# A transformer block in float32r pairs: the low parts of the feed-forward input weights come from an adding transfer instead of a subtraction

## The chip, the cores and the metric

The kernel runs on one core of a Trainium2 chip. A core has TensorE (PE, with its weight loads as PEld), VectorE (DVE), ScalarE (ACT), GpSimd (POOL) and SyncE (SP), which work from their own instruction queues, and 16 DMA engines. The metric is device time in microseconds: before the change the median of 3 runs is 1236.16 us (1234.19 to 1237.01).

## The reference

One block on 512 tokens with 1024 features in float32: a modulated norm, two kinds of attention (stick-breaking, retention), their gated mix, and a feed-forward part. The part that the change concerns:

```
hffn = modulate(rmsnorm(x, g_norm2[l]), shift2, scale2)
a, u = jnp.split(jnp.einsum('bsd,df->bsf', hffn, w_ffn_in[l]), 2, axis=-1)
x = x + gate2[:, None, :] * jnp.einsum('bsf,fd->bsd', jax.nn.silu(a) * u, w_ffn_out[l])
```

Each of a and u has 2816 columns, 22 tiles of 128.

## The kernel before, in words

Every large product is made of three matmuls for each tile. Weights and activations are split into a high part that fits the matmul's format (float32r) and a low part, the rest; `mm3` adds high x high, high x low and low x high. `gemm` does this for the 8 row tiles of a weight tile, which makes 24 matmuls in the order high, high, low for each row tile.

A weight tile is 128 x 1024 numbers (8 row tiles of 128 columns, 512 KB), packed on the host. `weight` (L204) fetches it: `load_raw` (L189) has SyncE's queue issue the load into one of three `raw` buffers; `split` (L194) has ACT copy raw to `whi` with rounding (L196), and DVE subtract, raw - whi, to `wlo` (L198). There are three buffers of `whi` and three of `wlo`, so a tile can be prepared only when PE has finished the third tile before it; the raw buffer comes free when both parts are made, and only then SyncE can issue the next load, in order.

The feed-forward part (the last loop of the kernel) runs in three chunks of 8, 8 and 6 tile pairs. For each pair i it fetches the tiles ("fa", i) and ("fu", i), here called fa and fu with the number, makes the products a and u in two of four PSUM banks, and `ff_act` makes Silu(a) x u: Silu on ACT (L764), the multiplication on DVE (L765), and the split into high and low activations, ACT then DVE (L196, L198). After each chunk come 8 products with w_ffn_out, whose tiles are fetched by `weight` too. Pair 0 runs by halves of 256 tokens, since the norm ahead of it (`norm2`, L753 to L757, and the reciprocal square root at L298 to L302) finishes the first half earlier than the second. Just before that, `add_residual` holds all three weight buffers until its last three tiles are done with both halves.

The order of instructions on each engine is made by the framework's scheduler, which moves what is ready sooner ahead; waits between engines are semaphores that it sets. GpSimd has work only in the earlier parts of the kernel.

Of the kernel before, what the change touches and what calls it, by code (L numbers as in the profile page):

```python
# [19 lines left out]
P = 128  # L20
# [17 lines left out]


def weight_plan():  # L40
    """(key, source, first row, row tiles, columns) of each packed weight tile, in order of use."""
    plan = []

    def add(key, src, r0, nk, cols):
        plan.append((key, src, r0, nk, cols))

    def rng(a, n):
        return [(a, n)]

    for kt in range(KT):  # L50
        add(("start", kt), "w_in", kt * P, 1, [(C_RQ, 256), (C_RK, 256), (C_RV, 256)])
    for g in range(4):
        for half in range(2):
            add(("sv", g, half), "w_in", half * 512, 4, rng(C_V + g * 256, 256))
        for p in (2 * g, 2 * g + 1):
            add(("sq", p), "w_in", 0, 8, rng(C_Q + p * P, P))
            add(("sk", p), "w_in", 0, 8, rng(C_K + p * P, P))
    for h in range(RH):
        for i in range(2):
            add(("rq", h, i), "w_in", 0, 8, rng(C_RQ + h * RK + i * P, P))  # L60
        for i in range(2):
            add(("rk", h, i), "w_in", 0, 8, rng(C_RK + h * RK + i * P, P))
        for i in range(2):
            for half in range(2):
                add(("rv", h, i, half), "w_in", half * 512, 4, rng(C_RV + h * RV + i * 256, 256))
        for i in range(4):
            add(("rg", h, i), "w_in", 0, 8, rng(C_RG + h * RV + i * P, P))
        for i in range(4):
            add(("pr", h, i), "w_proj_ret", h * RV, 4, rng(i * 256, 256))
    for i in range(8):  # L70
        add(("ps", i), "w_proj_sb", 0, 8, rng(i * P, P))
    for i in range(16):
        add(("br", i), "w_in", 0, 8, rng(C_BR + i * P, P))
    for i in range(8):
        add(("wo", i), "w_out", 0, 8, rng(i * P, P))
    for i in range(NF):
        add(("fa", i), "w_ffn_in", 0, 8, rng(i * P, P))
        add(("fu", i), "w_ffn_in", 0, 8, rng(DFF + i * P, P))
    for c, (k0, nk) in enumerate(FF_CHUNKS):
        for i in range(8):  # L80
            add(("fo", c, i), "w_ffn_out", k0 * P, nk, rng(i * P, P))
    return plan
# [4 lines left out]
PLAN = weight_plan()  # L87
WIDX = {e[0]: n for n, e in enumerate(PLAN)}

# column pairs of w_ada in order of use: (shift1, scale1) x 8, gate1 x 4, (shift2, scale2) x 8, gate2 x 4  # L90
ADA = (
    [(j, 8 + j) for j in range(8)]
    + [(16 + 2 * i, 17 + 2 * i) for i in range(4)]
# [1 line left out]
    + [(40 + 2 * i, 41 + 2 * i) for i in range(4)]  # L95
)

# smalls: columns of the packed small vectors
SM_BADA, SM_G1, SM_G2, SM_GF, SM_BB, SM_N = 0, 48, 56, 64, 72, 88

# (bank, column in the bank, first token, width) of the score block of 128 sources
GEO = ((0, 0, 0, 512), (1, 0, 128, 384), (2, 0, 256, 256), (2, 256, 256, 256))
BANKW = (512, 384, 512)

# [2 lines left out]
def kernel(  # L107
# [45 lines left out]
    def f(ap):  # L153
        return ap.bitcast(F32)

# [1 line left out]
    NCON = 2 * P + 48  # L157
    con = cpool.tile([P, NCON], F32, name="con")

# [25 lines left out]
    negones = cpool.tile([P, P], F32R, name="negones")  # L185
    nc.vector.tensor_scalar_mul(negones, ones, -1.0)

# [1 line left out]
    def load_raw(src, n, tag="raw"):  # L189
        raw = wpool.tile([P, WCOLS], F32, tag=tag, bufs=BUFS[tag], name=nm(tag))  # L190
        nc.sync.dma_start(raw[:, :n], src[:, :n])
        return raw

    def split(dst_hi, dst_lo, src, scale=1.0, eng=None):  # L194
        """dst_hi + dst_lo = src * scale, exactly (both parts fit float32r)."""
        nc.scalar.activation(dst_hi, src, AF.Copy, scale=scale)  # L196
        if isinstance(scale, float) and scale == 1.0:
            (eng or nc.vector).tensor_sub(dst_lo, src, f(dst_hi))  # L198
        else:
            nc.vector.scalar_tensor_tensor(  # L200
                dst_lo, src, scale, f(dst_hi), op0=ALU.mult, op1=ALU.subtract
            )

    def weight(key, eng=None):  # L204
# [8 lines left out]
        v = lambda t: t[:, :n].rearrange("p (k c) -> p k c", k=nk)  # L213
        return v(hi), v(lo)

    def mm(o, lhs, rhs, start, stop):
        nc.tensor.matmul(o, lhs, rhs, start=start, stop=stop, skip_group_check=True)  # L217

# [3 lines left out]
        mm(o, ll, rh, False, stop)  # L222

    def gemm(o, w, acts, start=True, stop=True, t0=0, t1=S):
        """o[e, t] (+)= sum over k of w[k, e] acts[k, t]."""
        hi, lo = w
        n = len(acts)
        for k in range(n):
            a = acts[k]
            mm3(o, hi[:, k, :], lo[:, k, :], a[:, 0, t0:t1], a[:, 1, t0:t1],  # L230
                start and k == 0, stop and k == n - 1)

# [1 line left out]
    mod = cpool.tile([P, 48], F32, name="mod")  # L234

    def ada(n):
        """columns of c_act @ w_ada + b_ada for the pair n, one value per partition."""
        pair_cols = []
        for half, c in enumerate(ADA[n]):
            if n < KT:  # L240
                raw = apool.tile([P, D], F32, tag="s", bufs=BUFS["s"], name=nm("sraw"))
                nc.sync.dma_start(raw, wada[2 * n + half])
            else:
                raw = load_raw(wada[2 * n + half], D, "araw")
            col = small(1)
            nc.vector.scalar_tensor_tensor(  # L246
                raw, raw, 1.0, cact, op0=ALU.mult, op1=ALU.mult, accum_out=col
            )
            nc.vector.tensor_add(mod[:, c : c + 1], col, sm[:, SM_BADA + c : SM_BADA + c + 1])  # L249
            pair_cols.append(mod[:, c : c + 1])  # L250
        return pair_cols

    def gain(scale, g):
        """(1 + scale) g"""
        a = small(1)
        nc.vector.scalar_tensor_tensor(a, scale, 1.0, g, op0=ALU.add, op1=ALU.mult)
        return a

# [1 line left out]
    def sumsq(x, acc, eng=None):  # L260
        """acc + x * x (a new tile when acc is None)."""
        sq = tmp()[:, : x.shape[-1]]
        nc.scalar.activation(sq, x, AF.Square)
        if acc is None:
            return sq
        (eng or nc.vector).tensor_add(acc, acc, sq)  # L266
        return acc

    def colsum(o, sq, first=True, last=True):
        """o[t, b] (+)= sum over features of sq[f, 128 b + t]."""  # L270
        for b in range(4):
            mm(o[:, b : b + 1], sq[:, b * P : (b + 1) * P], ones[:, 0:1],
               first and b == 0, last and b == 3)

    def rsqrt(v):
        """(y, c) with c * y = v ** -0.5 of a [128, 4] tile, to float32."""
        y, t, w = (small(4)[:, : v.shape[-1]] for _ in range(3))
        nc.vector.tensor_scalar(
            y.bitcast(I32), v.bitcast(I32), 1, None, op0=ALU.logical_shift_right
# [13 lines left out]
        return y, -k  # L293

    def rsqrt_act(v):
        """(y, c) with c * y = v ** -0.5, to float32; the scalar engine has the ln/exp tables."""
        y, t, w = (small(4)[:, : v.shape[-1]] for _ in range(3))
        nc.scalar.activation(w, v, AF.Ln)  # L298
        nc.scalar.activation(y, w, AF.Exp, scale=-0.5)
# [10 lines left out]
    last_diag = [None]  # L310

    def bcast(yc, o=None):
        """[128, 512] in PSUM: every row is the 512 values of c * y[128, 4] in token order."""
        y, cst = yc
        o = o or psz()
        for b in range(4):
# [10 lines left out]
        return rsqrt_act(v)  # L327

    def modulated(x, r, a, sh):
        """hi/lo pair of x * r * a + sh."""  # L330
        xn = tmp()
        nc.vector.tensor_mul(xn, x, r)  # L332
        nc.scalar.activation(xn, xn, AF.Identity, bias=sh, scale=a)
# [1 line left out]
        split(h[:, 0, :], h[:, 1, :], xn)  # L335
        return h

# [1 line left out]
    sq = None  # L339
    for j in range(KT):  # L340
        sq = sumsq(xts[j], sq)
# [35 lines left out]
    rope = table(consts[:, NCON : NCON + 2 * S])  # L377
    cosT, sinT = rope[:, 0:S], rope[:, S : 2 * S]

# [1 line left out]
    o_sb = [None] * 8  # L381
    sbq, sbk, sbv = {}, {}, {}

# [13 lines left out]
            sbk[2 * p + hf] = kt_[:, hf, :]  # L397

    def sb_v_store(g, banks):
        """per source block: [token, pair, (hi|lo|lo|hi)]: [vh|vl] for even heads, [vl|vh] for odd ones."""  # L400
        vt = [pair("v"), pair("v")]
        for b in range(4):
            t4 = vt[b // 2][:, b % 2, :].rearrange("p (r s d) -> p r s d", r=2, s=4)
# [16 lines left out]
        sb_v_store(g, banks)  # L420

    def causal(t, bank):
        """zero where the source is after the token."""
        op = ALU.is_ge

        def sel(ap, n, base):
# [66 lines left out]
        sb_head(2 * p)  # L493
        sb_head(2 * p + 1)

# [1 line left out]
    def ret_qk(h, banks=None):  # L497
        res = []
        for key in ("rq", "rk"):
# [14 lines left out]
        return res  # L514

    def tok_proj(banks, ws):
        """banks[b // 2][:, 256 (b % 2) + c] = sum over k of hs[k, 128 b + token] w[k, c]."""
        for half in range(2):
            hi, lo = weight(ws[half])
            for k in range(4):  # L520
# [96 lines left out]
                else:  # L617
                    nc.vector.tensor_add(p_ret[d], p_ret[d], o)

# [1 line left out]
    spill = dpool.tile([D, S], F32, name="spill")  # L621

    def gate(i):
# [95 lines left out]
    NSPLIT = 3  # L719

    def add_residual(get, gcol, acc, on_half):
        """x1[d] += gate[d] * product(d); the last tiles by halves of the tokens, so that the norm
        of the first half overlaps the products of the second."""
        for d in range(8 - NSPLIT):
            o = ps()
            gemm(o, *get(d))
# [31 lines left out]

    add_residual(lambda d: (weight(("wo", d)), ms), 16, None, norm2)

# [1 line left out]
    def ff_act(a, u, tag):  # L762
        t = tmp()
        nc.scalar.activation(t, a, AF.Silu)  # L764
# [13 lines left out]
    for c, (k0, nk) in enumerate(FF_CHUNKS):  # L778
        acts = []
        tag = "h" if c == 1 else "s"  # L780
        for i in range(k0, k0 + nk):
            a, u = ps(), ps()
            wa, wu = weight(("fa", i)), weight(("fu", i))
            if i == 0:
                for hv in HALVES:
                    for o, w in ((a, wa), (u, wu)):
# [78 lines left out]
```

## Time and profile before

| | |
|---|---|
| median of 3 runs | 1236.16 us |
| span of the profiled execution | 1233.6 us |
| PE busy | 1191.3 us, 97% |
| DVE busy | 717.9 us, 58% |
| ACT busy | 491.5 us, 40% |
| POOL busy | 32.0 us, 3% |
| feed-forward part | from about 856 us to the end |

The profile is that of one execution, and the times in its views are microseconds from the start of its span. A line such as `L196 ACT ACTIVATE whi<-raw` names the line of the kernel, the engine, the operation and the tiles that it writes and reads. In a timeline the first two numbers are the start and the length, xN joins N instructions, and the brackets give how long the engine was idle before and for what. The lines L194 to L202 are those of a helper that splits weights and activations alike, so a group is told by its tiles.

### The profile page before, as it was taken

The numbers are of one execution on the slowest core, as the hardware profiler recorded it, in microseconds if no ns is written. First come the engines' busy times: TensorE is split into PE (matmuls) and PEld (weight loads), VectorE is DVE, ScalarE is ACT, GpSimd is POOL, SyncE is SP. The second block draws the span as 40 slices with busy tenths as digits, with TensorE's granted clock in tenths as the row PEclk, the third lists the DMA queues.
The fourth block names the chain that finished last, engine by engine and source line by source line (L and its number), as shares of the span: only waits on it lengthen the run. The fifth ranks groups of instructions, "written<-read, shape, count | busy, mean of one in ns | idle before, by whom it ended". The sixth has DMA issues, their size and how long they took to land.

```text
span 1233.6 us, 15664 instructions
## 1 busy us (share of the span) xinstructions
PE 1191.3 (97%) x6190; PEld 1018.3 (83%) x6190; DVE 717.9 (58%) x1174; ACT 491.5 (40%) x764; POOL 32.0 (3%) x44
## 2 busy tenths in 40 slices
PE   3899999999999999999999999999999999999996
PEld 3788987898898888898988888888888888888886
DVE  6989886555554534377878887546433333333345
ACT  4344222332332322377677768324522223212232
POOL 1510000000000000000000000000000000000000
PEclk9999999999999999999999999999999999999998
DMA  9556771322233155525363625432323332332322
GB/s 338 182 201 189 239 256 52 103 86 69 86 95 103 52 137 154 149 95 133 90 146 98 162 64 158 154 103 64 108 96 92 103 96 92 103 96 93 94 77 69
DMA packets 48376, 150.37 MB, mean 122 GB/s; under 512 B 6064, under 2 KB 8240, under 8 KB 48304
## 3 DMA queue, kind: packets, MB, share of 16 engines
q1 hardware_dynamic: 48304, 149.38, 39.8%
q8 instruction: 48, 0.79, 0.3%
q14 instruction: 24, 0.20, 0.1%
HBM read 130.49 MB, written 4.19 MB: 109 GB/s over the span
## 4 chain that ended last, share of the span: by engine, by line
PE 86%; DVE 9%; DMA 3%; ACT 1%; issue 1%; POOL 0%; DVEq 0%; ACTq 0%
PE ps L217 73%; PE z L217 10%; DMA araw<-wada 3%; PE av L217 3%; DVE araw L246 1%; DVE sraw L246 1%; DVE mod L249 1%; DVE wlo L198 1%; DVE t L266 0%; DVE h L198 0%; DVE t L510 0%; DVE t L332 0%; DVE t L509 0%; DMA cact<-cvec 0%; DVE o L772 0%
## 5 line engine op out<-in xcount | busy, mean ns | idle before, releaser
L217 PE MATMUL ps<-h,whi 128*128 128x512 f32 (+1 forms) x1312 | 401.9, 385 | 6.8 <-ACT h L196 5.7
L196 ACT ACTIVATE whi<-raw 128x1024 fp32r<-128x1024 f32 (+1 forms) x190 | 197.6, 1041 | 484.5 <-PE ps L217 379.3
L198 DVE TENSOR_TENSOR wlo<-raw,whi 128x1024 fp32r<-128x1024 f32 (+1 forms) x182 | 220.4, 1211 | 161.4 <-ACT whi L196 159.4
L217 PEld LDWEIGHTS ps<-h,whi 128*128 128x128 f32 x1312 | 242.6, 189 | 55.0 <-ACT h L196 7.2
L217 PE MATMUL ps<-h,wlo 128*128 128x512 f32 (+1 forms) x656 | 251.6, 383 | 0.0
L217 PE MATMUL ps<-q,whi 128*128 128x512 f32 (+1 forms) x800 | 238.2, 381 | 0.4 <-ACT q L196 0.4
L217 PEld LDWEIGHTS ps<-q,whi 128*128 128x128 f32 x800 | 148.0, 188 | 29.2 <-ACT q L196 0.6
L217 PE MATMUL ps<-s,whi 128*128 128x512 f32 (+1 forms) x580 | 169.8, 376 | 0.0
L217 PE MATMUL ps<-q,wlo 128*128 128x512 f32 (+1 forms) x400 | 152.2, 381 | 2.1 <-DVE wlo L198 2.1
L217 PEld LDWEIGHTS ps<-h,wlo 128*128 128x128 f32 x656 | 123.8, 189 | 22.8
L217 PE MATMUL ps<-whi,h 128*128 128x256 f32 x704 | 129.6, 283 | 0.0
L217 PEld LDWEIGHTS ps<-s,whi 128*128 128x128 f32 x580 | 106.5, 188 | 19.7
L217 PEld LDWEIGHTS ps<-whi,h 128*128 128x128 f32 x704 | 110.8, 192 | 0.7
L217 PE MATMUL ps<-s,wlo 128*128 128x512 f32 (+1 forms) x290 | 109.0, 376 | 0.0
L217 PE MATMUL ps<-wlo,h 128*128 128x256 f32 x352 | 99.6, 283 | 0.3 <-DVE wlo L198 0.3
L198 DVE TENSOR_TENSOR s<-t,s 128x512 fp32r<-128x512 f32 (+1 forms) x126 | 79.4, 652 | 17.4 <-ACT s L196 17.2
L217 PEld LDWEIGHTS ps<-q,wlo 128*128 128x128 f32 x400 | 75.1, 188 | 16.7 <-DVE wlo L198 2.3
L196 ACT ACTIVATE s<-t 128x512 fp32r<-128x512 f32 (+1 forms) x126 | 72.8, 600 | 27.1 <-DVE t L599 23.2
L217 PEld LDWEIGHTS ps<-wlo,h 128*128 128x128 f32 x352 | 67.4, 192 | 0.9 <-DVE wlo L198 0.5
L217 PEld LDWEIGHTS ps<-s,wlo 128*128 128x128 f32 x290 | 54.6, 188 | 9.9
L765 DVE TENSOR_TENSOR t<-t,ps 128x512 f32<-128x512 f32 x22 | 15.1, 688 | 72.1 <-PE ps L217 71.4
L217 PE MATMUL z<-q,q 128*128 128x256 f32 (+2 forms) x224 | 45.0, 329 | 0.0
(130 smaller groups left out, 1087.5 us busy)
## 6 DMA issues: line engine op xcount, KB each, us to landing
raw<-wp SPq DMA_DIRECT2D x174, 512.0 KB, 3.6
araw<-wada SPq DMA_DIRECT2D x32, 512.0 KB, 4.5
sraw<-wada SPq DMA_DIRECT2D x16, 512.0 KB, 6.7
q<-qp SPq DMA_DIRECT2D x32, 256.0 KB, 3.7
raw<-wp SPq DMA_DIRECT2D x16, 384.0 KB, 3.2
o<-xT SPq DMA_DIRECT2D x16, 256.0 KB, 4.6
q<-qp SPq DMA_DIRECT2D x32, 128.0 KB, 3.2
spill<-t SPq DMA_DIRECT2D x8, 256.0 KB, 4.1
```

The costliest lines, as they stand in the source:

```text
L196: nc.scalar.activation(dst_hi, src, AF.Copy, scale=scale)
L198: (eng or nc.vector).tensor_sub(dst_lo, src, f(dst_hi))
L217: nc.tensor.matmul(o, lhs, rhs, start=start, stop=stop, skip_group_check=True)
L246: nc.vector.scalar_tensor_tensor(raw, raw, 1.0, cact, op0=ALU.mult, op1=ALU.mult, accum_out=col)
L249: nc.vector.tensor_add(mod[:, c : c + 1], col, sm[:, SM_BADA + c : SM_BADA + c + 1])
L765: nc.vector.tensor_mul(t, t, u)
```

## The change

For i of 1 or more the feed-forward loop fetches its two input tiles with a new function, `weight_dma`. ACT copies raw to `whi` as before; ACT then copies `whi` to `wlo` with its sign changed; then GpSimd's queue issues a transfer that adds raw to `wlo`, so that `wlo` = -whi + raw. Load, buffers and their numbers stay as they are, and so do pair 0 and the tiles of w_ffn_out. The other lines of the diff only empty docstrings and comments.

```diff
+    def weight_dma(key):
+
+        idx = WIDX[key]
+        _, _, _, nk, cols = PLAN[idx]
+        n = nk * sum(c for _, c in cols)
+        raw = load_raw(wp[idx], n)
+        hi = wpool.tile([P, WCOLS], F32R, tag="whi", bufs=BUFS["whi"], name=nm("whi"))
+        lo = wpool.tile([P, WCOLS], F32R, tag="wlo", bufs=BUFS["wlo"], name=nm("wlo"))
+        nc.scalar.activation(hi[:, :n], raw[:, :n], AF.Copy)
+        nc.scalar.activation(lo[:, :n], f(hi[:, :n]), AF.Copy, scale=-1.0)
+        nc.gpsimd.dma_start(f(lo[:, :n]), raw[:, :n], accum_op=ALU.add)
+        v = lambda t: t[:, :n].rearrange("p (k c) -> p k c", k=nk)
+        return v(hi), v(lo)
...
         for i in range(k0, k0 + nk):
             a, u = ps(), ps()
-            wa, wu = weight(("fa", i)), weight(("fu", i))
+            load = weight if i == 0 else weight_dma
+            wa, wu = load(("fa", i)), load(("fu", i))
```

## The prediction

> **What bounds the kernel now.** I read the page first. TensorE (PE) is busy 97% of the span and the chain that ended last consists mostly of its matmuls.
>
> ```profile
> span 1233.6 us, 15664 instructions
> PE 1191.3 (97%) x6190; PEld 1018.3 (83%) x6190; DVE 717.9 (58%) x1174; ACT 491.5 (40%) x764; POOL 32.0 (3%) x44
> ```
>
> Because an average over stages can mislead, the next view is the busy time by stretches of 50 us, for the stretch in which the feed-forward begins and for one in its middle (columns: window, length, then busy time and count of PE, weight loads, VectorE, ScalarE, GpSimd, then granted clock, DMA share, GB/s).
>
> ```profile
> 850.00:900.00 50.00, 47.46 (x280) 42.09 (x280) 29.24 (x60) 28.57 (x55) 0.00 (x0) 1.00 0.31 95
> 1000.00:1050.00 50.00, 50.00 (x222) 41.39 (x221) 17.48 (x19) 14.25 (x18) 0.00 (x0) 1.00 0.32 98
> ```
>
> In the middle PE has no idle time at all, the clock is fully granted, VectorE (DVE) is busy for a third and ScalarE (ACT) for less. The chain of waits says the same: from 865.62 us on it is matmuls alone.
>
> ```profile
> 865.62 134.58 PE ps L217 x615
> ...
> 999.97 215.66 PE ps L217 x983
> ```
>
> So the stage is bound by matmuls, which the change doesn't touch. It can only lose time by making PE wait for a low part; it can win at most what PE idles at the start of the stage, 50.00 - 47.46 = 2.54 us.
>
> How much earlier is a low part ready than PE needs it? One turn of the stage, from the timeline of all engines (start, length, engine, line, operation):
>
> ```profile
> 1002.05 1.06 ACT L196 ACTIVATE whi<-raw 128x1024 fp32r<-128x1024 f32 x1 [3.90 <-PE ps L217]
> 1003.07 0.63 ACT L196 ACTIVATE h<-t 128x512 fp32r<-128x512 f32 x1
> 1003.14 1.23 DVE L198 TENSOR_TENSOR wlo<-raw,whi 128x1024 fp32r<-128x1024 f32 x1
> 1004.39 5.82 SPq L191 DMA_DIRECT2D raw<-wp  x2
> ...
> 1007.54 1.06 ACT L196 ACTIVATE whi<-raw 128x1024 fp32r<-128x1024 f32 x1 [3.84 <-PE ps L217]
> 1008.50 0.58 ACT L764 ACTIVATE t<-ps 128x512 f32<-128x512 f32 x1
> ...
> 1012.98 1.06 ACT L196 ACTIVATE whi<-raw 128x1024 fp32r<-128x1024 f32 x1 [3.89 <-issue]
> 1013.18 0.19 PEld L217 LDWEIGHTS ps<-q,wlo 128*128 128x128 f32 x1
> ```
>
> ACT makes a high part at the moment at which PE lets go of one of the three buffers, and this recurs every (1012.98 - 1002.05) / 2 = 5.46 us, the time of 24 matmuls. The tile whose high part starts at 1002.05 is used two tiles later: PE turns to it at about 1012.9 and loads its first low block at 1013.18. Its low part is finished at 1003.14 + 1.23 = 1004.37, so it is 8.8 us early. At 1004.39 SyncE's queue issues the load that waited for that raw buffer.
>
> **The change part by part.** It concerns 42 tiles (i = 1 to 21, two each). In the stretch from 883 to 1215 us the two operations cost, the last columns being busy time and mean ns:
>
> ```profile
> L198 DVE TENSOR_TENSOR wlo<-raw,whi 128x1024 fp32r<-128x1024 f32 (+1 forms) x62 | 73.8, 1191 | 78.7 <-ACT whi L196 77.1
> L196 ACT ACTIVATE whi<-raw 128x1024 fp32r<-128x1024 f32 (+1 forms) x62 | 64.1, 1034 | 239.8 <-PE ps L217 164.4 <-issue 75.4
> ```
>
> (1) *Removed:* 42 subtractions of 1.23 us on DVE, 52 us. DVE is idle for two thirds of this stage, so this is worth nothing, except once at the start (the faster rival).
>
> (2) *Added on ACT:* 42 sign-changing copies, costed at the 1.06 us of the copy beside them, 45 us. ACT works 14.25 us of 50 now and would work about 24; what hides it is ACT's idle time (3.9 us before each high part). Queued behind it are the Silu (L764) and the split of the activations (L196), each late by up to 1.06 us. PE needs the split of tile pair i only in the later product, and a Silu's bank two pairs later, so I cost this at zero.
>
> (3) *Added on GpSimd and the DMA engines:* 42 transfers of 512 KB within the on-chip memory which read raw, read lo and write lo. GpSimd (POOL) has no work in this stage, so nothing is queued behind their wait on ACT. The trace has no transfer issued from GpSimd and none that adds. The nearest rows (KB each, us from issue to landing; the third is from the window 900 to 1200 us):
>
> ```profile
> q<-qp SPq DMA_DIRECT2D x32, 256.0 KB, 3.7
> q<-qp SPq DMA_DIRECT2D x32, 128.0 KB, 3.2
> ...
> raw<-wp SPq DMA_DIRECT2D x48, 512.0 KB, 3.5
> ```
>
> Call the time from issue to landing D. The lower end is the load of the same size, 3.5 us. For copies within the on-chip memory, 128 KB more costs 0.5 us, so a plain one of 512 KB would take 3.7 + 2 x 0.5 = 4.7 us. If reading the destination costs as much as a second whole transfer, D is 9.4, and with some issue time on GpSimd 10 us is the upper end. I take 7, the middle between one pass and two, since the second read can share the start and the end of the transfer but not the bytes.
>
> As an estimate from the Trainium skill: "DMA: Bandwidth & Descriptors", section "Anatomy of one DMA — SWDGE (gpsimd) path", fits a transfer issued from GpSimd as 2.0 us plus its bytes over 436e3 per us, which is 3.2 us for 512 KiB; and "Collectives: The Full Stack", section "The bandwidth ceiling: the fold count and why AG ≠ RS ≠ AR", says that an adding transfer runs at half rate because it reads two sources, not because adding costs anything, which doubles the second term: 2.0 + 2.4 = 4.4 us. No row here shows such a transfer; by this figure the stall worked out in (5) would be 1.2 to 3.1 us in place of 3.8 to 5.7.
>
> (4) *The steady state.* High part at 1002.05, done at 1003.11, sign-changed copy done at 1004.2 (or 1004.8 if a Silu of 0.58 goes first). PE wants the result at 1013.18. So D may be 8.4 to 9.0 us before PE notices; 7 is hidden, with 1.4 to 2 us to spare. The raw buffer is let go at 1004.2 + 7 = 1011.2 in place of 1004.39, so the next load, queued on SyncE behind that wait, lands at about 1011.2 + 3.5 = 1014.7; its high part is due at 1002.05 + 3 x 5.46 = 1018.4. Also hidden. Zero at D = 7.
>
> The rate must hold too. How fast do the engines copy on chip and load? Two windows (the last columns are DMA share and GB/s), the first with copies within the chip, the second with loads:
>
> ```profile
> 701.10:704.90 3.80, 3.80 (x18) 3.11 (x18) 3.77 (x8) 2.02 (x5) 0.00 (x0) 1.00 0.69 170
> ...
> 1004.40:1009.80 5.40, 5.40 (x26) 4.46 (x25) 1.74 (x2) 1.55 (x2) 0.00 (x0) 1.00 0.32 97
> ```
>
> A load of 512 KB keeps the 16 engines busy for 0.32 x 5.46 = 1.7 us. At 170 / 0.69 = 246 GB/s a plain copy takes 2.1 us. With a second read that overlaps the write the adding transfer stays near 2.1, without any overlap it takes 4.3. Together with the load that is 3.8 to 6.0 us for every 5.46 us. I take the middle, 4.9, which fits.
>
> (5) *The start of the stage.* Here the cover is thinner, since the first feed-forward pair runs by halves of the tokens and both its buffers come free late, one just after the other. ACT and then PE:
>
> ```profile
> 858.00 1.99 ACT L196 ACTIVATE whi<-raw 128x1024 fp32r<-128x1024 f32 x2
> 859.89 0.19 ACT L298 ACTIVATE sm<-sm 128x2 f32<-128x2 f32 x1
> ...
> 871.88 1.06 ACT L196 ACTIVATE whi<-raw 128x1024 fp32r<-128x1024 f32 x1 [1.20 <-PE ps L217]
> 872.96 1.28 ACT L764 ACT_TABLE_LOAD   x1
> 874.25 0.60 ACT L764 ACTIVATE t<-ps 128x512 f32<-128x512 f32 x1
> 874.75 1.05 ACT L196 ACTIVATE whi<-raw 128x1024 fp32r<-128x1024 f32 x1
> ...
> 869.29 0.40 PE L217 MATMUL ps<-q,wlo 128*128 128x512 f32 x1
> ...
> 877.18 0.19 PEld L217 LDWEIGHTS ps<-q,wlo 128*128 128x128 f32 x1
> ```
>
> The two high parts from 858.00 on are those of fu0 and fa1. That of fa1 is done at 860.0, its copy at about 861.4 (behind the two short operations at 859.89), the sum at 868.4 with D = 7. PE first uses that low part at 869.29: just hidden, by 0.9 us. Tile fu1 is the one that isn't. Its high part can't start before 871.88, when PE lets go of fa0, and its low part is wanted at 877.18, after only 5.3 us. If the sign-changed copy follows at once, the transfer starts at 874.0 and lands at 881.0: PE waits 3.8 us. If the table load and the Silu go first, it starts at 875.9 and lands at 882.9: 5.7 us. In the program the first pair's Silu stands ahead of these weights, but its table load and the copy become ready at the same time, so both orders are possible; I take the middle, 4.7 us. Late next is fa2: its high part moves from 874.75 to about 876, its copy ends near 878.5, its sum lands at 885.5, and PE, itself delayed, wants it at 877.18 + 5.46 + 4.7 = 887.3. Hidden. From there on (4) holds, and the products between the chunks use the old way and give the buffers time to catch up.
>
> *The sum:* 0 - 0 + 0 + 4.7 = +4.7 us on the profiled 1233.6 us, so 1238.3 us. The median of the runs shown, 1236.16, is 2.56 us above this profile's span; with it the prediction is 1240.9 us.
>
> **The rivals.**
>
> *Sustained stall.* From D = 9.0 on, each loop through the three buffers is too long: 2.1 us on ACT, D, then 5.2 us until PE gives the buffer back, hence a tile takes (7.3 + D) / 3. With D = 10 that is 5.77 in place of 5.46, over some 36 tiles (the first two or three of each chunk start with full buffers) 11 us, plus a start of 6.8 to 8.7: about 1255 us. If the engines' rate decides at 6.0 us for each tile, it is 0.54 x 40 = 22 us and the start: 1263 us. An addition slower than its reads would cost more still, and nothing in this trace limits that. For it: the margin in (4) is under 2 us and the operation has no row. Against it: both ends need two full passes without overlap.
>
> *Covered.* With D at 5.5 or less and the copy right behind the high part, fu1 is late by 874.0 + 5.5 - 877.18 = 2.3 us or less, and nothing else is. The time is 1236 to 1238.5 us, which can't be told from no change. For it: a plain 512 KB copy by the rows takes 4.7. Against it: ACT's order may cost 1.9 us by itself.
>
> *Faster.* At the start DVE's subtraction for fa1 stands in the middle of the second half's norm:
>
> ```profile
> 861.04 1.22 DVE L198 TENSOR_TENSOR wlo<-raw,whi 128x1024 fp32r<-128x1024 f32 x1
> 862.17 0.15 DVE L301 TENSOR_TENSOR sm<-sm,sm 128x2 f32<-128x2 f32 x1
> ```
>
> Without it the norm is 1.2 us earlier, and PE, which idles 2.54 us in this stretch, could use that. It decides if the sum for fu1 is there by 877.18 (D under 3.2, or another order of PE's work), and is worth 2.54 us at most: 1233.6 us. Against it: most of that idle time is a wait for fa0's own low part, which is made as before.
>
> *The change doesn't do what it says:* the low part is still written once by a compute engine, only by ACT instead of DVE, and then a second time by the transfer. That relieves no engine that sets the end, and is contained in the sum.
>
> **How the numbers follow.** Differences within 0.2%, 2.5 us, can't be told from no change. One stall at the start, 2.5 to 6 us: 0.45. Sustained stall: 0.30. Covered: 0.19. Faster by more than 2.5 us: 0.06. Slower has 0.45 + 0.30 = 0.75, faster 0.06, the rest is the same. The likeliest case alone lies between 1238.7 and 1243 us. The range begins at 1235.5, inside the covered case, and ends at 1265, just above the sustained case with two full passes; about 0.1 is left out on each side.
>
> **What would show it.** The landing time of the adding transfers in the list of DMA issues gives D: under 8.4 us the middle of the stage keeps 50.0 us of PE in 50, above 9 there are waits for a DMA before most tiles. The start must show one wait of PE of 4 to 6 us at the first low block of fu1, near 877 us. The DMA share in the middle should be 0.7 to 1.0 in place of 0.32, ACT's busy time near 24 us in 50, DVE's near 6 us. The prediction is wrong if D is beyond 9, if the DMA share reaches 1, or if PE doesn't wait at fu1.

## The result and the profile after

The changed kernel takes 1236.91 us (median of 20 runs, 1234.98 to 1239.14) against 1233.90 us for the kernel before (20 runs, 1232.02 to 1237.01). The ratio is 1.0022, 95% interval 1.0015 to 1.0028: slower by 2.7 us (1.9 to 3.5). The forecast was slower by 4.7 us, so the direction was right and the size too large. The three runs from which the forecast took its base had a median 2.3 us above that of the 20, which puts the predicted time, 1240.9 us, further off than the predicted difference.

The page, and the busy time by stretches of 50 us (same columns as before):

```profile
span 1235.4 us, 15813 instructions
PE 1192.1 (96%) x6190; PEld 1018.0 (82%) x6190; DVE 667.6 (54%) x1132; ACT 532.8 (43%) x806; POOL 68.4 (6%) x86
```

```profile
850.00:900.00 50.00, 45.14 (x252) 39.14 (x251) 18.74 (x46) 31.48 (x54) 6.17 (x7) 0.97 0.59 139
...
1000.00:1050.00 50.00, 50.00 (x223) 41.39 (x222) 6.91 (x10) 23.48 (x28) 7.86 (x10) 1.00 0.86 189
```

DVE has 50 us less work and ACT 41 us more. In the middle PE is as full as before, although the DMA engines now work 0.86 of the time in place of 0.32. All that the feed-forward part loses is lost between 850 and 900 us.

The place, from the timelines of ACT, GpSimd and PE:

```profile
868.68 1.06 ACT L224 ACTIVATE whi<-raw 128x1024 fp32r<-128x1024 f32 x1 [1.21 <-PE ps L231]
869.76 1.28 ACT L778 ACT_TABLE_LOAD   x1
871.05 0.60 ACT L778 ACTIVATE t<-ps 128x512 f32<-128x512 f32 x1
871.55 1.05 ACT L225 ACTIVATE wlo<-whi 128x1024 fp32r<-128x1024 f32 x1
...
872.91 0.86 POOL L226 DMA_DIRECT2D wlo<-raw  x1 [13.19 <-ACT wlo L225]
...
877.53 0.50 PE L231 MATMUL ps<-q,wlo 128*128 128x512 f32 x1 [2.68 <-DMA wlo<-raw]
...
877.52 0.19 PEld L231 LDWEIGHTS ps<-q,wlo 128*128 128x128 f32 x1 [3.11 <-DMA wlo<-raw]
```

This is tile fu1. ACT did the table load and the Silu ahead of the sign-changing copy, the later of the two orders considered. The transfer went out at 872.91 and released PE at 877.48, after 4.57 us; the weight load had waited 3.11 us, the matmul behind it 2.68. (Weight loads run ahead of the matmuls, so the two waits differ; below, each number says which it is.) The rest of the stage, from the list of DMA issues between 900 and 1200 us:

```profile
raw<-wp SPq DMA_DIRECT2D x49, 512.0 KB, 4.1
wlo<-raw POOLq DMA_DIRECT2D x35, 512.0 KB, 5.8
```

There the transfers run beside loads and take 5.8 us, the loads 4.1 in place of 3.5. Both stay hidden: a high part begun at 1003.47 in this trace has its copy ready at 1006.08, its sum about 6 us later, and is wanted 11.1 us after its beginning, at 1014.6, so some 2.4 us are left. The slowest of the 42 transfers took 8.3 us, and PE waited for none but that of fu1.

Behind the wait the trace shows one thing more, the granted clock (the number ahead of the DMA share; 1.00 is full speed):

```profile
878.00:880.00 2.00, 2.00 (x8) 1.57 (x7) 0.00 (x0) 0.00 (x0) 0.69 (x1) 0.68 1.10 168
880.00:882.00 2.00, 2.00 (x6) 1.52 (x6) 0.00 (x0) 0.00 (x0) 0.00 (x0) 0.50 0.90 289
882.00:884.00 2.00, 2.00 (x10) 1.66 (x9) 0.00 (x0) 0.00 (x0) 0.00 (x0) 0.97 1.09 213
```

From about 1 us after the wait, for some 3.5 us, PE ran at about half speed (6 matmuls in 2 us in place of 10 or 11). By the granted clock that is 2 x (0.32 + 0.50 + 0.03) = 1.7 us. So this one profile lost more in the feed-forward part than the timed runs did. Both kernels wait once at the first low block of fa0; counted from the end of that wait to the end of the span, before took 1233.6 - 858.38 = 375.22 us and after 1235.4 - 855.68 = 379.72 us:

```profile
858.38 0.39 PE L217 MATMUL ps<-q,wlo 128*128 128x256 f32 x1 [2.14 <-DVE wlo L198]
```

```profile
855.68 0.39 PE L231 MATMUL ps<-q,wlo 128*128 128x256 f32 x1 [2.15 <-DVE wlo L198]
```

That is 4.5 us more. The wait at fu1 is 3.1 of it and the clock 1.7; against them stand 0.4 us that PE waits in the kernel before, at 865.62, for the norm's split, and no longer in the changed one:

```profile
865.62 0.86 PE L217 MATMUL ps<-q,whi 128*128 128x256 f32 x4 [0.40 <-ACT q L196]
```

The parts ahead of the wait at fa0, which the change doesn't touch, happened to be 2.7 us shorter. Most of that is the clock again: in the profile before it fell near 190 us, behind a wait of PE for DVE of 2.75 us, and in the one after it didn't (before, then after):

```profile
180.00:200.00 20.00, 17.25 (x89) 15.11 (x88) 13.43 (x25) 5.07 (x8) 2.27 (x8) 0.91 0.40 124
```

```profile
180.00:200.00 20.00, 18.88 (x103) 16.14 (x101) 13.76 (x24) 5.70 (x9) 2.29 (x8) 1.00 0.32 105
```

So each of the two spans holds one fall of the clock, and the one behind fu1 adds next to nothing to the 1.8 us between them.

### The profile page after: what moved, and what is told of

Its sections match the earlier page's. It is cut to its first block, busy times and chain, and to the rows that moved or that the text cites. A ratio compares the mean times of both kernels' runs of the same rounds, so it can differ in the third digit from the quotient of the medians.

```text
span 1235.4 us, 15813 instructions
## 1 busy us (share of the span) xinstructions
PE 1192.1 (96%) x6190; PEld 1018.0 (82%) x6190; DVE 667.6 (54%) x1132; ACT 532.8 (43%) x806; POOL 68.4 (6%) x86
## 4 chain that ended last, share of the span: by engine, by line
PE 83%; DVE 10%; DMA 4%; issue 1%; ACT 1%; POOL 0%; DVEq 0%; POOLq 0%
PE ps L231 71%; PE z L231 9%; DMA araw<-wada 4%; PE av L231 2%; DVE araw L260 2%; DVE sraw L260 1%; DVE mod L263 1%; DVE wlo L198 1%; DVE t L280 1%; DVE h L198 0%; DVE t L524 0%; DVE t L346 0%; DVE t L523 0%; DMA cact<-cvec 0%; DMA wlo<-raw 0%
## 5 line engine op out<-in xcount | busy, mean ns | idle before, releaser
L196 ACT ACTIVATE whi<-raw 128x1024 fp32r<-128x1024 f32 (+1 forms) x148 | 153.1, 1035 | 332.1 <-PE ps L231 303.4
L198 DVE TENSOR_TENSOR wlo<-raw,whi 128x1024 fp32r<-128x1024 f32 (+1 forms) x140 | 168.8, 1206 | 93.6 <-ACT whi L196 92.3
L224 ACT ACTIVATE whi<-raw 128x1024 fp32r<-128x1024 f32 x42 | 44.5, 1060 | 119.8 <-PE ps L231 119.8
L226 POOL DMA_DIRECT2D wlo<-raw x42 | 36.3, 864 | 742.1 <-DVE sm L314 461.3
```

Source lines behind the costliest of these rows:

```text
L224: nc.scalar.activation(hi[:, :n], raw[:, :n], AF.Copy)
L226: nc.gpsimd.dma_start(f(lo[:, :n]), raw[:, :n], accum_op=ALU.add)
```

## The experiments

Theory A: the loss is the one wait at fu1 and what follows from it. Theory B: it is spread over the 42 tiles. Theory C: ACT's additional copies are to blame. The ratios are to the kernel before, run beside each on the same chip, with 95% intervals.

**Everything but pair 1.**

```diff
-            load = weight if i == 0 else weight_dma
+            load = weight if i <= 1 else weight_dma
```

> The transfer from pair i = 2 on, 40 tiles of 42; pair 1 by subtraction as before. Theory A (the whole loss is PE's one wait at the first low block of fu1 and the reduced clock behind it): no wait of PE in the feed-forward part beyond that at its first tile, ratio to before 1.000 within 0.001. Theory B (the loss is spread over the stage, about 0.07 us for each tile, from busier DMA engines or a busier ACT): 40/42 of the loss stays, ratio 1.002.

Measured: 0.9999 (0.9989 to 1.0010), and no new wait of PE longer than 0.3 us. The 40 transfers of the steady part cost nothing that can be measured. B falls.

**Pair 1 alone.**

```diff
-            load = weight if i == 0 else weight_dma
+            load = weight_dma if i == 1 else weight
```

> The transfer for pair i = 1 only, 2 tiles of 42. Theory A: the whole loss, ratio 1.002 to 1.003, PE waits about 3 us at the first low block of fu1, and the granted clock falls to about 0.5 for some 3.5 us after it. Theory B: 2/42 of the loss, ratio 1.000.

Measured: 1.0019 (1.0011 to 1.0028). Two tiles of 42 carry the loss, within the interval. The wait looks different, because the scheduler put matmuls of the next tile between those of fu1:

```profile
876.76 0.50 PE L231 MATMUL ps<-q,wlo 128*128 128x512 f32 x1 [0.53 <-DVE wlo L198]
...
879.11 0.50 PE L231 MATMUL ps<-q,wlo 128*128 128x512 f32 x1 [1.16 <-DMA wlo<-raw]
```

It is two waits, 1.7 us together for the matmuls and 0.96 + 1.59 = 2.6 us for the weight loads. The expected fall of the clock behind fu1 did not come; in this run it came earlier (0.67 between 856 and 860 us, behind the wait at fa0).

**Without the transfer.**

```diff
-        nc.gpsimd.dma_start(f(lo[:, :n]), raw[:, :n], accum_op=ALU.add)
```

> All 42 sign-changing copies on ACT, but no adding transfer (the low part is left at minus the high part). Theory A: fu1's low part is there when ACT is done, 1.9 us after the start of the transfer in the changed kernel less the landing time, so PE doesn't wait; ratio 1.000 within 0.001. Theory C (ACT's extra copies cost the time by themselves): the ratio stays at 1.002.

Measured: 0.9995 (0.9986 to 1.0004), no wait at fu1. (This kernel leaves out the addition of raw, so its low parts and its result are not those of the block.) ACT's 42 additional copies cost nothing. C falls.

**The sign on DVE.**

```diff
-        nc.scalar.activation(lo[:, :n], f(hi[:, :n]), AF.Copy, scale=-1.0)
+        nc.vector.tensor_scalar_mul(lo[:, :n], f(hi[:, :n]), -1.0)
```

> The sign-changing copy on DVE instead of ACT, so that it needn't queue behind the Silu's table load and the Silu. Theory A: for fu1 the transfer starts about 1.5 to 2 us earlier, PE waits 1.1 to 1.6 us in place of 3.1, and no fall of the clock follows; ratio 1.001. Theory B: 1.002, as the transfers are the same.

Measured: 0.9997 (0.9987 to 1.0008). GpSimd issues fu1's transfer 2.1 us after ACT began the high part (868.73), in place of 872.91 - 868.68 = 4.2:

```profile
870.82 0.86 POOL L226 DMA_DIRECT2D wlo<-raw  x1 [11.29 <-DVE wlo L225]
```

```profile
875.43 0.50 PE L231 MATMUL ps<-q,wlo 128*128 128x512 f32 x1 [0.79 <-DMA wlo<-raw]
```

With the same 42 transfers, but this one 2.1 us earlier, the matmul waits 0.8 us in place of 2.7, and the loss is gone within the interval. The weight load still waits 1.2 us, which is too little for these runs to show in the time.

**Table load ahead.**

```diff
             split(hf[j][:, 0, hv], hf[j][:, 1, hv], xn)
+        if n == 1:
+            tc.keep_in_program_order(nc.scalar.preload_act_table_set("silu_and_others"))
```

> The table load of the Silu put ahead, behind the last activation of the norm, where ACT is idle. ACT's order is then Silu, high part of fu1, split of the first pair's product, sign-changing copy of fu1, so that this copy ends about 0.7 us earlier after PE's release of the buffer: PE waits about 2.4 us at fu1, ratio 1.001 to 1.002. If ACT's order at this place isn't the cause, 3.1 us.

Measured: 1.0018 (1.0008 to 1.0028). The wait of the weight load at fu1's low block is shorter than expected:

```profile
879.24 0.19 PEld L231 LDWEIGHTS ps<-q,wlo 128*128 128x128 f32 x1 [1.76 <-DMA wlo<-raw]
```

The scheduler put six high blocks ahead of it in place of four, and the last two of them waited 0.46 us for their high part on ACT; the two waits make 2.2 us, near the 2.4 expected. (One more wait for a transfer, 0.41 us of a weight load, came at 894.94.) So ACT's order at this place has its share in the wait; the interval of the ratio is too wide to tell by how much the time falls with it.

**Half transfers.**

```diff
-        nc.gpsimd.dma_start(f(lo[:, :n]), raw[:, :n], accum_op=ALU.add)
+        for s0 in (0, n // 2):
+            c = slice(s0, s0 + n // 2)
+            nc.gpsimd.dma_start(f(lo[:, c]), raw[:, c], accum_op=ALU.add)
```

> Each adding transfer cut into two of 256 KB. If the transfer's own time for its bytes sets the wait at fu1, PE can go on after the first half, which lands about 0.9 us sooner: it waits about 2.2 us, ratio 1.001 to 1.002. If the landing time is all fixed cost, the wait stays at 3.1 us and the ratio at 1.002.

Measured: 1.0013 (1.0004 to 1.0021). From the chain of waits, and PE's timeline:

```profile
873.96 3.81 DMA wlo<-raw
```

```profile
877.82 0.50 PE L233 MATMUL ps<-q,wlo 128*128 128x512 f32 x1 [1.91 <-DMA wlo<-raw]
```

The first half released PE after 3.81 us in place of 4.57, and the matmul's wait is shorter by the same 0.8 us (1.91 for 2.68). So, as an estimate from these two sizes, 256 KB of adding cost 0.76 us, and about 3.05 us of the 4.57 don't depend on the size; that the second half, issued behind the first, doesn't slow it is assumed.

**The changed kernel again.** Its source is the same.

> The changed kernel once more. Theory A: PE waits 2.5 to 3.5 us at the first low block of fu1, no other new wait, ratio 1.0015 to 1.003. Open is the clock: if its fall belongs to this wait, the granted clock goes to about 0.5 behind it again; if it depends on where the wait falls, it can stay away, or come after the 2.1 us wait at fa0, as in the run with the sign on DVE.

Measured: 1.0037 (1.0024 to 1.0051), above the first series, though the intervals overlap. Wait and transfer repeat to 0.01 us, but the clock stayed full behind fu1 and fell behind the wait at fa0:

```profile
878.86 0.50 PE L231 MATMUL ps<-q,wlo 128*128 128x512 f32 x1 [2.69 <-DMA wlo<-raw]
```

```profile
856.00:860.00 4.00, 4.00 (x25) 4.00 (x24) 2.74 (x9) 2.33 (x5) 1.01 (x1) 0.63 0.63 153
```

**More latency for each tile.**

```diff
-        nc.scalar.activation(lo[:, :n], f(hi[:, :n]), AF.Copy, scale=-1.0)
+        nc.scalar.activation(lo[:, :n], f(hi[:, :n]), AF.Copy, scale=-2.0)
+        nc.gpsimd.tensor_add(lo[:, :n], f(lo[:, :n]), f(hi[:, :n]))
```

> Same transfers, but ACT makes minus twice the high part and GpSimd adds the high part before it issues the transfer: some 3.7 us of latency more for each low part, no DMA work more. In the changed kernel a low part is ready about 2.5 us before PE wants it in the steady state. If the loop through the three buffers sets the limit (tile time = (7.3 + latency of GpSimd and transfer) / 3), a tile takes about 5.9 us in place of 5.46 and the ratio is 1.010 to 1.020. If the margin is larger than 4 us, only the start is longer by 3.7 us: ratio 1.005.

Measured: 1.0165 (1.0144 to 1.0187), about 20 us. The size is in the expected span, but the reason is another one. GpSimd's addition took 2.4 us and not 3.7, so with the median landing of this run, 6.0 us, the low part's loop alone would have held: (7.3 + 2.7 + 6.0) / 3 = 5.3 us for a tile. ACT's timeline shows, at one place, who was late:

```profile
999.82 1.06 ACT L224 ACTIVATE whi<-raw 128x1024 fp32r<-128x1024 f32 x1 [3.29 <-PE ps L232]
...
1017.58 1.06 ACT L224 ACTIVATE whi<-raw 128x1024 fp32r<-128x1024 f32 x1 [4.28 <-DMA raw<-wp]
```

The high part at 1017.58 waited for its raw tile. That load takes the buffer of the tile begun at 999.82, which the adding transfer keeps until it has landed; SyncE may issue the load only then. Round this loop it took 17.76 us for three tiles, 5.92 for one, in place of 5.46. Here the transfer took 6.76 us and the load 5.9; with the medians, 6.0 and 4.1, this loop too would have held. Between 880 and 1215 us ACT's high part waited for a raw load seven times, 27.5 us in all, so the loop closes where a load and a transfer are slow, and not at every tile. And it isn't all of the 20 us: about half is lost ahead of 900 us, where PE idles 4.3 us more than in the kernel before and the granted clock is 0.90 on average over 50 us. That the raw loop is the rest is not shown.

**Two transfers for each tile.**

```diff
-        nc.scalar.activation(lo[:, :n], f(hi[:, :n]), AF.Copy, scale=-1.0)
+        nc.scalar.activation(lo[:, :n], f(hi[:, :n]), AF.Copy, scale=-2.0)
         nc.gpsimd.dma_start(f(lo[:, :n]), raw[:, :n], accum_op=ALU.add)
+        nc.gpsimd.dma_start(f(lo[:, :n]), f(hi[:, :n]), accum_op=ALU.add)
```

> Two adding transfers for each tile, one after the other (minus twice the high part, plus raw, plus the high part). If only latency counts, with 5.8 us for each: a tile takes (7.3 + 11.6) / 3 = 6.3 us, ratio about 1.03. If the rate of the DMA engines decides, with 2.9 us of all 16 engines for each adding transfer and 1.7 for a load: 7.5 us for each tile, ratio about 1.065.

Measured: 1.1312 (1.1289 to 1.1334), far above both. GpSimd's timeline:

```profile
908.19 1.17 POOL L226 DMA_DIRECT2D wlo<-raw  x1
916.63 0.86 POOL L227 DMA_DIRECT2D wlo<-whi  x1 [7.27 <-DMA wlo<-raw]
917.17 1.21 POOL L226 DMA_DIRECT2D wlo<-raw  x1
925.60 0.86 POOL L227 DMA_DIRECT2D wlo<-whi  x1 [7.22 <-DMA wlo<-raw]
```

The second addition must wait until the first has landed, and it waits at the head of GpSimd's queue, with the next tile's first transfer behind it. So each tile costs one whole landing and the issues, 917.17 - 908.19 = 9.0 us. Neither the loop through the buffers nor the engines' rate was the limit (the DMA share was 0.81 between 900 and 950 us), but the order of a queue. The run tells nothing on which of those two would come first.

**The other wait, at fa0.** In the kernel before:

```diff
-            wa, wu = weight(("fa", i)), weight(("fu", i))
+            wa = weight(("fa", i), nc.gpsimd) if i == 0 else weight(("fa", i))
+            wu = weight(("fu", i))
```

> The kernel before with one edit: the subtraction for tile fa0 on GpSimd, which is idle, in place of DVE, where it queues behind the norm and makes PE wait 2.14 us at the first low block of the feed-forward part. If that wait is DVE's queue alone, PE starts the stage 1 to 2 us earlier: ratio 0.9985 to 0.999. If the norm's own splits set the pace, 1.000.

Measured: 0.9996 (0.9986 to 1.0005), not told from no change. PE's timeline:

```profile
856.13 0.39 PE L231 MATMUL ps<-q,whi 128*128 128x256 f32 x1 [0.54 <-DVE q L198]
857.30 0.58 PE L231 MATMUL z<-ones,t 128*128 128x1 f32 x4 [0.32 <-DVE t L280]
859.60 0.39 PE L231 MATMUL ps<-q,wlo 128*128 128x256 f32 x1 [0.39 <-DVE wlo L198]
...
864.24 0.85 PE L231 MATMUL ps<-q,whi 128*128 128x256 f32 x4 [1.24 <-ACT q L196]
```

The kernel before waits 2.14 us here and 0.40 at 865.62. In their place stand four smaller waits, 2.49 us together, three for the norm's work on DVE and ACT and one, of 0.39 us, for the low part of fu0 on DVE. So PE is held up here by more than the one subtraction. No version that was tried beats the kernel before.

## Why the prediction was right, and where it was wrong

*What bounds the stage; removing 42 subtractions; 42 more copies on ACT.* Right: 50.0 of 50 us of PE in the middle, and the runs without the transfer and without pair 1 are level with before. ACT's 23.5 us and DVE's 6.9 us in 50 are close to the 24 and 6 that were forecast.

*The steady state.* Right, with a D of 5.8 in place of 7. The rate was well taken: the DMA share of 0.86 is 4.7 us of 5.46, where 4.9 had been said.

*The start.* Place and mechanism were right: fu1 alone, released late, and the copy behind the table load and the Silu. The step that failed is the size of one term, D, where the prediction says "I take 7, the middle between one pass and two". The transfer that PE waited for took 4.57 us, a little under the 4.7 that a plain copy was reckoned to take. At the order that came about, the wait was forecast as 5.7 us at D = 7; with 4.57 the same sum gives 5.7 - 2.4 = 3.3, and the weight load waited 3.1. As one pass fitted the rows and the second was a guess, the middle was too high. The estimate of 4.4 us from the Trainium skill's "DMA: Bandwidth & Descriptors", section "Anatomy of one DMA — SWDGE (gpsimd) path", and "Collectives: The Full Stack", section "The bandwidth ceiling: the fold count and why AG ≠ RS ≠ AR" (which states the half rate for the reducing transfers of a ReduceScatter), came close to the 4.57; its division doesn't agree, since the half transfers show 3.05 us fixed and 1.5 us for 512 KB where the estimate has 2.0 and 2.4.

*The order on ACT.* Taking the middle of two possible orders, 4.7 us, gave an answer that belongs to neither. That it lay nearer to the 3.1 than the 5.7 of the order that came about was luck: this error made up for part of the one in D.

*Sustained stall.* It didn't happen, as D stayed under 8.4. Its formula left out the raw buffer: with more latency the loop through raw, transfer and load can close where the formula's doesn't, as at 1017.58 in that run.

*Covered.* One of its two conditions held, D under 5.5, and the other, the copy right behind the high part, didn't. The measured 1236.91 us lies in its span, 1236 to 1238.5, and outside the 1238.7 to 1243 called likeliest, in part because the base was too high. That its loss can't be told from no change was wrong too: 20 runs of each tell 2.7 us from none.

*Faster.* Of the 2.54 us that PE idled, 0.40, a wait for the norm's split, is gone in the changed kernel's profile; the wait for fa0's low part stayed, 2.15 for 2.14, as the prediction held against this rival.

*Not foreseen:* the fall of the clock behind a wait.

## What to carry to other kernels

When an operation with slack in the steady state is made longer, the first turns of the stage must be counted one by one: there the buffers come free late and in a burst, one-time work such as a table load stands in the queue, and one tile of 42 made the difference here. A transfer that reads a buffer holds it until it has landed, so the loop through that buffer and its next load has to be checked beside the loop through the result. And a transfer that waits for another one blocks everything behind it on the issuing queue.

## What the runs showed of the hardware

The granted clock of PE can fall to about half for some 3.5 us behind a wait of only 1.7 to 2.8 us, and it needn't. All the kernels with fa0's subtraction on DVE have the same wait of 2.1 us at fa0. In the profiles of before, of the run from pair 2 on, of that without the transfer and of that with the table load ahead, the clock stayed full behind it; in those of the half transfers, of pair 1 alone, of the sign on DVE, of the repetition, of the run with more latency and of that with two transfers it fell, and in the first profile of the changed kernel it fell behind fu1 instead. The table takes the start of the first low block of fa0 and the span from each profile; the waits are those of the weight loads at fu1 and the tiles mixed with it (0.96 + 1.59 for pair 1 alone, 0.46 + 1.76 with the table load ahead).

| profile | start | span | from there to the end | more than before | of it waits at fu1 | rest | clock fell behind |
|---|---|---|---|---|---|---|---|
| before | 858.38 | 1233.6 | 375.2 | | | | (near 190 us) |
| without the transfer | 857.57 | 1232.3 | 374.7 | -0.5 | 0 | -0.5 | (near 190 us) |
| everything but pair 1 | 860.39 | 1235.9 | 375.5 | 0.3 | 0 | 0.3 | (near 190 us) |
| table load ahead | 858.01 | 1235.3 | 377.3 | 2.1 | 2.2 | -0.1 | (near 190 us) |
| sign on DVE | 854.59 | 1231.6 | 377.0 | 1.8 | 1.2 | 0.6 | fa0 |
| half transfers | 855.28 | 1234.1 | 378.8 | 3.6 | 2.3 | 1.3 | fa0 |
| changed, again | 855.53 | 1235.1 | 379.6 | 4.4 | 3.1 | 1.2 | fa0 |
| pair 1 alone | 855.58 | 1234.9 | 379.3 | 4.1 | 2.6 | 1.5 | fa0 |
| changed | 855.68 | 1235.4 | 379.7 | 4.5 | 3.1 | 1.4 | fu1 |

The wait accounts for the difference to within 0.5 us where the clock stayed full, and 0.6 to 1.5 us come on top where it fell. Before and the run from pair 2 on have the 0.4 us for the norm's split as well, which the others lack; with it the rest is at most 0.3 us where the clock stayed full and 1.0 to 1.9 us where it fell, about the 1.7 us that the fall took in the changed kernel.

Each of these nine profiles has one fall ahead of 1200 us, that of the kernel before too. In the four that have none at fa0 or fu1 it came near 190 us, at a wait of PE for DVE of 1.7 to 3.5 us (granted clock 0.83 to 0.91 on average over the 20 us from 180); in the other five that wait was 1.5 us or less, and the clock stayed full there. The length of the wait doesn't decide alone: the run with fa0's subtraction on GpSimd waits 1.96 us near 190 us and has no fall. What does decide isn't shown.

The Trainium skill, "TensorE: Matmul & The Clock Gate", section "Part 1: The HAM clock gate (the "warmup" mystery)", puts the fall behind an idle window of about 3.4 us and the recovery after as long a busy one; the idle time needed was shorter here, and the recovery agrees but for one profile, that of the run from pair 2 on, in which the clock was at half from 190.9 to 197.6 us.

It shows in the times too: of 76 runs of the kernel before, those with a mean granted clock of 0.993 have a median of 1236.4 us, those with 0.997 one of 1232.9. That is more than the effect of the change, and makes single profiles of two such kernels hard to compare as a whole. Whether the changed kernel falls more often than the kernel before, and whether that explains why its two series gave 1.0022 and 1.0037, stays open.
